# Hybrid attention/recurrence block on one core: the opening with x also laid out transposed, and four direct chunks

## The chip, the cores and the metric

The kernel runs on one core of one Trainium2 chip. A core has four engines with their own in-order instruction queues: PE (TensorE, matrix products into PSUM), DVE (VectorE, elementwise work and sums along a row), ACT (ScalarE, functions of one input with a scale and a bias per partition) and POOL (GpSimd), and SP, which only issues DMAs. The engines wait for each other through semaphores. The metric is device microseconds of one execution, the median over several runs.

## The reference

The block takes x (1024 tokens by 1024 features, fp32). In short:

```python
mod = c @ w_ada + b_ada                      # shift, scale, gate: 1024 each
h = rmsnorm(x, norm_g) * (1 + scale) + shift
proj = h @ w_in                              # 1024 x 6656
q, k, v, g_attn, xr, g_rnn, m_attn, m_rnn = split(proj)
q, k = partial_rope(q, pos), partial_rope(k, pos)
y_attn = sliding_window_attention_with_sinks(q, k, v) * silu(g_attn)
xr = causal_depthwise_conv(xr)
y_rnn = rg_lru(xr, pos) * silu(g_rnn)
merged = sigmoid(m_attn) * (y_attn @ w_ap) + sigmoid(m_rnn) * (y_rnn @ w_rp)
x = x + gate * (merged @ w_out)
return rmsnorm(x, final_g)
```

with rmsnorm(x, g) = x / sqrt(mean(x^2) + eps) * g, the mean over a token's features.

## The kernel before

Every fp32 operand of a large product is split into a high part (`h`, rounded to the format fp32r) and a low part (`l`, the rest), and the product is three: hh, hl, lh. A weight half (128 x 512) is loaded as `r`, ACT casts it to `wh` (L101, or L103 with a scale), and DVE takes the rest `wl` (L107, L109). The products need h transposed, features on the partitions, in 8 chunks of 128 features (`kc` 0 to 7), each as `hh[kc]` and `hl[kc]` over 1024 tokens in two halves.

The opening (L178 to L360) makes them. x comes in eight tiles of 128 tokens; for each, the sum of squares (four on ACT, L309, four on DVE, L311), the root (L316), the reciprocal, and the scaling of the tile (L318). PE transposes the scaled tiles (L323, 64 of them) and ACT copies them to `xT[kc]` (L325). Then for each `kc`: `modulate` (DVE, two products of a w_ss tile with the broadcast row c, each with a running sum, L220, and two small steps) gives the scale `gsc` and the shift `mods` of the 128 features; DVE applies them to `xT[kc]` (L344); ACT rounds (L347); DVE takes the rest (L349). As each chunk comes, PE adds its part of three direct output chunks (`starts`: two chunks of k and the first of q, L168), 6 matmuls of 512 columns each. In this part a scheduler sets the order of each engine's instructions, and it also pulls in matmuls of V (L1259 to L1261, 192 narrow ones in all).

From L363 on the order is that of the program text. GpSimd makes differences of the tiles `xT` (`differences`, L378), `make_operands` rounds them (L386), and then come "pairs": two output chunks by a Strassen-like scheme with 7 products of 12 matmuls (84, L505) where two direct chunks need 96. A planner with costs per step (`Load`, `background`, the slots of `at_slot`) spreads the pairs' preparation and the recurrence's steps over the pairs' products. The order of the pairs is the list `pairs`: Q[1] (query chunks), MA[0] (the first gate pair of attention), Q[2], and so on, 23 in all. Between the opening and the pairs stand the rope of k and of the first q chunk (`rope_a`, `rope_b`), V, and the second chunk of q (48 matmuls, L168).

## Time and profile before

| what | value |
|---|---|
| median of 3 runs | 944.52 us (944.16 to 946.5) |
| profiled execution | 944.47 us, span 942.5 us |
| PE busy | 908.1 us (96%) |
| DVE busy | 688.8 us (73%) |
| ACT busy | 528.8 us (56%) |
| POOL busy | 89.7 us (10%) |
| mean DMA rate | 174 GB/s |

The span is the time from the first to the last recorded instruction, and the profiled execution's own time lies 2.0 us above it. Busy shares are means over stages with different limits. In the timeline rows the columns are start, duration, engine, line, operation, output<-input, shapes and count, and in brackets the idle time of the engine just before, with what ended it. An engine's operations overlap a little at their ends, so that the distance from start to start is less than the duration shown.

### The profile page before, as it was taken

Reading aid. Unit: us, or ns where it says so; the run is one execution under the profiler, and the core shown is the slowest. Engines: PE = TensorE matmul, PEld = TensorE weight load, DVE = VectorE, ACT = ScalarE, POOL = GpSimd, SP = SyncE. Lnnn points to the kernel's source line nnn. Section 1 sums busy time; section 2 is a strip of 40 time slices with the busy share of each in tenths; the row PEclk is TensorE's granted clock in tenths of the full one; section 3 lists DMA queues with packets and bytes.
Section 4 is the critical chain, followed back from the end, with each engine's and each line's share of the span. In section 5 each row is a group of like instructions: output and inputs, shape, how many; then the busy total and the mean of one; then the engine's idle time right before and its main releaser. Section 6 shows DMA issues by size and latency. Waiting matters only on the chain.

```text
span 942.5 us, 12419 instructions
## 1 busy us (share of the span) xinstructions
PE 908.1 (96%) x4261; PEld 750.6 (80%) x4261; DVE 688.8 (73%) x1068; ACT 528.8 (56%) x1036; POOL 89.7 (10%) x129
## 2 busy tenths in 40 slices
PE   5899999999999999999999999989999999999997
PEld 3689777788888788888888778867888888887886
DVE  7977798876668955984688677888999737656522
ACT  7434654455556755866585775877888632212311
POOL 1056000000000000000000000233333300000000
PEclk9999999999999999999999999999999999999999
DMA  8923565753332433352334237897666286436321
GB/s 312 370 68 152 184 223 202 268 189 125 112 112 96 139 136 100 133 212 80 122 112 168 100 134 261 278 342 251 215 198 187 67 304 219 168 118 235 128 79 67
DMA packets 84275, 164.19 MB, mean 174 GB/s; under 512 B 12771, under 2 KB 33251, under 8 KB 84214
## 3 DMA queue, kind: packets, MB, share of 16 engines
q1 hardware_dynamic: 83350, 161.09, 49.8%
q0 software_dynamic: 720, 2.07, 0.6%
q8 instruction: 33, 0.54, 0.2%
q14 instruction: 28, 0.23, 0.1%
q10 hardware_dynamic: 144, 0.26, 0.1%
HBM read 114.00 MB, written 49.78 MB: 174 GB/s over the span
## 4 chain that ended last, share of the span: by engine, by line
PE 75%; ACT 4%; DMA 4%; DVE 4%; issue 2%; SPq 0%; POOL 0%; DVEq 0%; ACTq 0%
PE bk L505 39%; PE rp L168 12%; PE rp L1500 5%; PE pgate L778 5%; PE pmain L1500 4%; PE pmain L168 4%; PE s_ps L1016 3%; PE pv L1088 3%; PE pt L1054 1%; DMA dv<-dv_d 1%; DMA ks<-k_d 1%; DMA r<-w_rp 1%; ACT wh L101 1%; DMA r<-w_main 1%; DVE nl L390 1%
## 5 line engine op out<-in xcount | busy, mean ns | idle before, releaser
L505 PE MATMUL bk<-nh,wl 128*128 128x512 f32 x368 | 143.7, 391 | 2.0 <-DVE wl L107 1.9
L505 PE MATMUL bk<-nh,wh 128*128 128x512 f32 x368 | 143.4, 390 | 0.0
L505 PE MATMUL bk<-nl,wh 128*128 128x512 f32 x368 | 143.2, 389 | 0.0
L107 DVE TENSOR_TENSOR wl<-r,wh 128x512 fp32r<-128x512 f32 x108 | 79.1, 736 | 16.5 <-ACT wh L101 16.5
L101 ACT CAST wh<-r 128x512 fp32r<-128x512 f32 x108 | 66.5, 618 | 33.5 <-DMA r<-w_ap 11.3
L505 PEld LDWEIGHTS bk<-nh,wl 128*128 128x128 f32 x368 | 69.1, 188 | 17.7 <-DVE wl L107 3.1
L505 PEld LDWEIGHTS bk<-nh,wh 128*128 128x128 f32 x368 | 69.1, 188 | 15.2 <-ACT wh L103 0.9
L505 PEld LDWEIGHTS bk<-nl,wh 128*128 128x128 f32 x368 | 69.1, 188 | 14.3
L505 PE MATMUL bk<-hh,wl 128*128 128x512 f32 x184 | 71.7, 390 | 0.4 <-DVE wl L107 0.4
L505 PE MATMUL bk<-hl,wh 128*128 128x512 f32 x184 | 71.6, 389 | 0.0
L505 PE MATMUL bk<-hh,wh 128*128 128x512 f32 x184 | 71.6, 389 | 0.0
L107 DVE TENSOR_TENSOR wl<-ws,wh 128x512 fp32r<-128x512 f32 x80 | 54.1, 683 | 4.0 <-ACT wh L101 4.0
L101 ACT CAST wh<-ws 128x512 fp32r<-128x512 f32 x80 | 48.2, 616 | 4.8 <-DVE ws L527 3.0
L1040 ACT ACTIVATE p<-p,small 128x129 f32<-128x129 f32 x128 | 50.1, 400 | 0.0
L59 POOL DMA_DIRECT2D yh_d<-yh x1 | 0.6, 583 | 482.3 <-ACT yh L835 482.3
L505 PE MATMUL bk<-hha,wl 128*128 128x512 f32 x92 | 36.4, 395 | 5.9 <-DVE wl L107 4.4
L505 PEld LDWEIGHTS bk<-hh,wl 128*128 128x128 f32 x184 | 34.5, 188 | 7.9 <-DVE wl L107 0.8
L505 PEld LDWEIGHTS bk<-hh,wh 128*128 128x128 f32 x184 | 34.5, 188 | 7.2
L505 PEld LDWEIGHTS bk<-hl,wh 128*128 128x128 f32 x184 | 34.5, 188 | 7.1
L1016 PE MATMUL s_ps<-ks,qs 128*128 128x256 f32 (+1 forms) x256 | 37.5, 289 | 0.0
L1517 ACT ACTIVATE o<-xo 128x1024 f32<-128x1024 f32 (+2 forms) x10 | 8.9, 889 | 48.4 <-DVE xo L1516 48.4
L505 PE MATMUL bk<-hla,wh 128*128 128x512 f32 x92 | 35.9, 390 | 0.0
(338 smaller groups left out, 2231.7 us busy)
## 6 DMA issues: line engine op xcount, KB each, us to landing
r<-w_main SPq DMA_DIRECT2D x100, 256.0 KB, 4.0
wada<-w_ss SPq DMA_DIRECT2D x16, 512.0 KB, 8.6
qs<-q_d SPq DMA_DIRECT2D x16, 512.0 KB, 5.4
ks<-k_d SPq DMA_DIRECT2D x24, 192.0 KB, 4.1
xt<-x SPq DMA_DIRECT2D x8, 512.0 KB, 7.2
q_d<-rhi SPq DMA_DIRECT2D x16, 256.0 KB, 3.5
q_d<-rlo SPq DMA_DIRECT2D x16, 256.0 KB, 3.3
wg<-w_gate SPq DMA_DIRECT2D x8, 512.0 KB, 5.0
```

The source lines that it names most:

```text
L101: A.copy(dst[0][:], src)
L107: V.tensor_tensor(out=dst[1][:], in0=src, in1=f32(dst[0][:]), op=ALU.subtract)
L168: mm = T.matmul(ps[hf], ww, xx[kc][hf], start=(kc == 0 and ww is w_h and xx is xh), stop=(kc == KC - 1 and xx is xl))
L390: V.tensor_tensor(out=nl[t][:], in0=xT[t][:], in1=f32(nh[t][:]), op=ALU.subtract)
L505: W["pe"] = T.matmul(ps, ww[:, c], b[kc][xx_], start=(first and kc == 0 and i == 0), stop=(kc == 3 and i == 2), skip_group_check=not first)
L778: W["pe"] = T.matmul(ps[:, SL[hf]], ww[:, c0:c0 + P], xx_[:, SL[hf]], start=(ic == 0 and i == 0), stop=(ic == 1 and i == 2))
L1016: W["pe"] = T.matmul(o, qs[:, j, qc], ks[:, b, k0 + (0 if n else P):k0 + 256], start=(b == 0), stop=(b == 1))
L1040: A.activation(px[:, j, :], px[:, j, :], AF.Exp, bias=sm[:, 0, j:j + 1], accum_out=sm[:, 1, j:j + 1])
L1054: W["pe"] = T.transpose(pt[:, j, :], px[:, j, 0:P], ident[:])
L1088: W["pe"] = T.matmul(pv[:], b, m[:].rearrange("p j q -> p (j q)"), start=(i == 0), stop=(i == len(prods) - 1))
L1500: T.matmul(ps[:, sl], lhs[k][th][:, ts_], w[:, sl], start=(k == 0 and w is h_ and lhs is mh), stop=(k == KC - 1 and lhs is ml))
L1517: A.activation(o[:, sl], xo[:, sl], AF.Square, accum_out=fs[:, i:i + 1])
```

## The change

The input x is also handed over transposed (`x_t`), and w_ss gets a last column that holds b_ada, so that its rows have 1025 values and the sum gives the modulation with its bias. The whole opening is now in the order of the program text. The x tiles in token order serve for the sums of squares alone, all on ACT. The roots of four tiles are taken in one instruction; the reciprocals are spread over the partitions by PE (`spread`: each column of reciprocals broadcast as one operand and the identity as the other) and copied to `r_bc`. PE runs 14 and 6 dummy products (`warm`). `xT[kc]` is loaded from x_t and multiplied by `r_bc` on DVE (`norm`); ACT makes the rounded h directly from it with scale and bias (`high_h`), and then the affine tile in place (`affine`); DVE takes the rest (`low_h`). Four chunks (k twice, the two of q's first group) are multiplied as h arrives. The first gate pair MA[0] leaves the list of pairs and is multiplied directly (2 x 48 matmuls) behind V; GpSimd's differences come in another order of tiles, behind the whole opening. The third block of the recurrence (`hb` 2) loses its pauses of one slot between steps, and XR[3] is now three places behind XR[2], where MA[3] stood between.

The core of the diff:

```diff
+        load_ss(0)
+        for i in range(8):
+            load_xt(i)
+        load_t(0)
+        for i in range(3):
+            load_wh(i, 0)
+        load_ss(1)
+        load_t(1)
+        load_wh(3, 0)
+        load_t(2)
+        load_ss(2)
...
         def modulate(kc):
             for a in range(2):
-                jk = sp.tile([P, D], BF16, tag="junk2", name="jk")
+                jk = sp.tile([P, D + 1], BF16, tag="junk2", name="jk")
                 V.scalar_tensor_tensor(out=jk[:], in0=wada[kc, a][:], scalar=1.0, in1=c_bc[:],
                                        op0=ALU.mult, op1=ALU.mult,
                                        accum_out=mods[:, a * 8 + kc:a * 8 + kc + 1])
-            shf = mods[:, kc:kc + 1]
-            g1 = gsc[:, kc:kc + 1]
-            V.scalar_tensor_tensor(out=g1, in0=mods[:, 8 + kc:9 + kc],
-                                   scalar=bsc1[:, kc:kc + 1], in1=pcol(PK_NG, kc),
-                                   op0=ALU.add, op1=ALU.mult)
-            V.tensor_tensor(out=shf, in0=shf, in1=pcol(PK_BSH, kc), op=ALU.add)
-            return g1, shf
-
-        def load_start(i):
-            w = load_w(w_main[i], 0.125 if i == 2 else 1.0)
-            starts.append((w, new_ps() if i < 2 else bk[2:]))
+            V.scalar_tensor_tensor(out=gsc[:, kc:kc + 1], in0=mods[:, 8 + kc:9 + kc],
+                                   scalar=1.0, in1=pcol(PK_NG, kc), op0=ALU.add,
+                                   op1=ALU.mult)
...
+        def square(i):
+            junk = sp.tile([P, D], BF16, tag="junk", name="junk")
+            A.activation(junk[:], xt[i], AF.Square, accum_out=ss[:, i:i + 1])
+
+        def root_of(hf):
+            r1 = rr[:, hf * 4:hf * 4 + 4]
+            V.tensor_scalar(out=r1, in0=ss[:, hf * 4:hf * 4 + 4], scalar1=1.0 / D, scalar2=EPS,
+                            op0=ALU.mult, op1=ALU.add)
+            A.activation(r1, r1, AF.Sqrt)
+
+        def spread(hf):
+            r1 = rr[:, hf * 4:hf * 4 + 4]
+            V.reciprocal(r1, r1)
+            for j in range(4):
+                T.matmul(bk[2 + hf][:, j * P:(j + 1) * P],
+                         r1[:, j:j + 1].to_broadcast([P, P]), ident[:], start=True, stop=True)
+
+        def gather(hf):
+            A.copy(r_bc[:, SL[hf]], bk[2 + hf])
+
+        main = [new_ps(), new_ps()]
+
+        def warm(n):
+            for i in range(n):
+                T.matmul(main[1][0][:, :P], ident[:], ident[:], start=True, stop=True)
+
+        def norm(kc):
+            for sl in SL if kc == 0 else [slice(0, S)]:
+                V.tensor_tensor(out=xT[kc][:, sl], in0=xT[kc][:, sl], in1=r_bc[:, sl],
+                                op=ALU.mult)
+
+        def high(i, h):
+            W0[i, h] = slot()
+            cast(W0[i, h], halfw[i, h], 0.125 if i > 1 else 1.0)
+
+        def low(i, h):
+            rest(W0[i, h], halfw[i, h], 0.125 if i > 1 else 1.0)
+
+        def high_h(kc):
+            for o, i in ([(hh[kc][hf], xT[kc][:, SL[hf]]) for hf in range(2)] if kc < 4 else
+                         [(hall[kc][0], xT[kc][:])]):
+                A.activation(o, i, AF.Identity, scale=gsc[:, kc:kc + 1],
+                             bias=mods[:, kc:kc + 1])
+
+        def affine(kc):
+            A.activation(xT[kc][:], xT[kc][:], AF.Identity, scale=gsc[:, kc:kc + 1],
+                         bias=mods[:, kc:kc + 1])
+
+        def low_h(kc):
+            for o, i, h in ([(hl[kc][hf], xT[kc][:, SL[hf]], hh[kc][hf]) for hf in range(2)]
+                            if kc < 4 else [(hall[kc][1], xT[kc][:], hall[kc][0])]):
+                V.tensor_tensor(out=o, in0=i, in1=f32(h), op=ALU.subtract)
...
+        modulate(0)
+        pieces, a00 = angles()
+        for i in range(4):
+            square(i)
+        root_of(0)
+        square(4)
+        spread(0)
+        warm(14)
+        square(5)
+        gather(0)
+        turns(pieces, a00)
+        for i in range(6, 8):
+            square(i)
+        root_of(1)
+        spread(1)
+        warm(6)
+        gather(1)
+        norm(0)
+        high(0, 0)
+        high_h(0)
+        starts = [([], ps) for ps in (main[0], main[1], bk[2:], bk[:2])]
+
+        def half(i, h):
+            if (i, h) not in W0:
+                high(i, h)
+            low(i, h)
+            starts[i][0].append(W0[i, h])
+
+        half(0, 0)
+        high(1, 0)
+        high(2, 0)
+        half(1, 0)
+        half(2, 0)
+        affine(0)
+        low_h(0)
+        half(3, 0)
         for kc in range(KC):
-            if kc == 0:
-                load_start(1)
-                load_start(2)
-            else:
-                load_ss(kc)
-            with tc.issue_after(xsc.ins):
-                g1, shf = modulate(kc)
-            V.tensor_scalar(out=xT[kc][:], in0=xT[kc][:], scalar1=g1, scalar2=shf,
-                            op0=ALU.mult, op1=ALU.add)
-            for hf in range(2):
-                last = A.copy(hh[kc][hf], xT[kc][:, SL[hf]])
-            for hf in range(2):
-                V.tensor_tensor(out=hl[kc][hf], in0=xT[kc][:, SL[hf]], in1=f32(hh[kc][hf]),
-                                op=ALU.subtract)
-            if kc < 6:
+            if kc + 1 < KC:
+                modulate(kc + 1)
+                norm(kc + 1)
+                high_h(kc + 1)
+                affine(kc + 1)
+                low_h(kc + 1)
+            if kc < 4:
+                load_wh(kc, 1)
+            if kc + 3 < KC:
+                load_t(kc + 3)
+                load_ss(kc + 3)
+            if kc == 4:
+                rv = [load_half(w_v[i // 2][:, SL[i % 2]]) for i in range(4)]
+            if kc == 1:
+                table()
+            if kc == 2:
+                half(0, 1)
+            if kc == 4:
+                for i in range(1, 4):
+                    half(i, 1)
+            for terms in ("h", "l") if kc < 3 else ():
                 for w, ps in starts:
-                    mm_k(ps, w, kc, terms="h")
+                    mm_k(ps, w, kc, terms=terms)
+            if kc in (3, 4, 5):
                 for w, ps in starts:
-                    mm_k(ps, w, kc, terms="l")
-        done = None
+                    mm_k(ps, w, kc)
         for w, ps in starts:
-            with tc.issue_after(done.ins) if done else nullcontext():
-                for kc in (6, 7):
-                    done = mm_k(ps, w, kc)
-
-
-    order = ExitStack()
-    ET = mybir.EngineType
-    order.enter_context(tc.manual_schedule(engines={ET.PE, ET.Activation, ET.DVE, ET.Pool,
-                                                    ET.SP}))
+            for kc in (6, 7):
+                mm_k(ps, w, kc)
...
-                todo.extend(step + ([slots(1)] if hb < 3 else []))
+                todo.extend(step + ([slots(1)] if hb < 2 else []))
...
-    pairs = [Q[1], MA[0], Q[2], MA[1], Q[3],
-             XR[0], GR[0], GR[1], XR[1], MA[2], GR[2], MR[0], XR[2], MR[1], MR[2], MA[3],
+    pairs = [Q[1], MA[1], Q[2], MA[2], Q[3],
+             XR[0], GR[0], GR[1], XR[1], MA[3], GR[2], MR[0], XR[2], MR[1], MR[2],
...
+    for i in (3, 0, 1, 2):
...
+    kept = aside(0)
+    wv = [split(slot(), r) for r in rv]
+    ps_v = new_ps()
+    v_product(ps_v, 0)
+    rm = [load_half(w_main[C_MA + i][:, SL[j]]) for i in range(2) for j in range(2)]
     now(*part(1, rope_b, k_d))
+    now(*[rope_a(lambda hf=hf: kept[hf], hf, k_d) for hf in range(2)])
+    ps_w = new_ps()
+    v_product(ps_w, 1)
+    v_store(ps_v, 0)
     now(*part(2, rope_a, q_d[0]))
-    ps_v = new_ps()
-    v_product(ps_v, 1)
-    wq.append(split(slot(), rq[1], 0.125))
-    v_store(bk[:2], 0)
-    make_operands(0)
-    make_operands(1)
-    begin(-4, -3, -2)
-    make_operands(2)
-    v_store(ps_v, 1)
+    make_operands(3)
+    wm = [split(slot(), r) for r in rm]
+    begin(-6)
+    now(*part(3, rope_b, q_d[0]))
+    begin(-5)
+    v_store(ps_w, 1)
+    for c, ps in enumerate((bk[2:], new_ps())):
+        for kc in range(KC):
+            mm_k(ps, wm[2 * c:2 * c + 2], kc)
+        if c == 0:
+            begin(-4)
+            make_operands(0)
+            begin(-3)
+            make_operands(1)
+            begin(-2)
+            make_operands(2)
+        for hf in range(2):
+            b = blk()
+            A.activation(b, ps[hf], AF.Tanh, scale=0.5)
+            dma(sma_d[c][:, SL[hf]], b)
```

How it moves instructions, at three places. First DVE in the loop over the chunks; `hla`, `hlb` are the low halves of a chunk, `jk` the junk output of a modulation product, a higher number is a later chunk. Before, from the affine step of chunk 1 to that of chunk 2:

```order
L344 TENSOR_SCALAR xT<-xT,gsc,mods 128x1024
L220 SCALAR_TENSOR_TENSOR jk,mods<-wada,c_bc 128x1024
L228 TENSOR_TENSOR mods<-mods,pk_t 128x1
L349 TENSOR_TENSOR hla_164<-xT,hha_162 128x512
L225 SCALAR_TENSOR_TENSOR gsc<-mods,bsc_219,pk_t 128x1
L349 TENSOR_TENSOR hlb_165<-xT,hhb_163 128x512
L220 SCALAR_TENSOR_TENSOR jk,mods<-wada,c_bc 128x1024
L344 TENSOR_SCALAR xT<-xT,gsc,mods 128x1024
```

After, chunk 1 and the beginning of chunk 2 (L360 is `norm`, L383 `low_h`):

```order
L244 SCALAR_TENSOR_TENSOR jk,mods<-wada,c_bc 128x1025
L244 SCALAR_TENSOR_TENSOR jk,mods<-wada,c_bc 128x1025
L247 SCALAR_TENSOR_TENSOR gsc<-mods,pk_t 128x1
L360 TENSOR_TENSOR xT<-xT,r_bc 128x1024
L383 TENSOR_TENSOR hla_164<-xT,hha_162 128x512
L383 TENSOR_TENSOR hlb_165<-xT,hhb_163 128x512
L244 SCALAR_TENSOR_TENSOR jk,mods<-wada,c_bc 128x1025
```

Before, a modulation product of the next chunk stood between the step that ACT waits for (L344) and the one that waits for ACT (L349); now nothing stands between L360 and L383.

Second ACT in the same loop. Before, behind the transposed copies:

```order
L347 CAST hha_166<-xT 128x512
L347 CAST hhb_167<-xT 128x512
L347 CAST hha_170<-xT_191 128x512
L347 CAST hhb_171<-xT_191 128x512
L103 ACTIVATE wh<-r 128x512
L101 CAST wh<-r 128x512 x2
L347 CAST hh_174<-xT 128x512 x2
```

After, from chunk 3 to chunk 6 (L373 is `high_h`, L377 `affine`, L101 and L103 weight casts):

```order
L373 ACTIVATE hha_170<-xT,mods,gsc 128x512
L373 ACTIVATE hhb_171<-xT,mods,gsc 128x512
L377 ACTIVATE xT<-xT,mods,gsc 128x1024
L101 CAST wh<-r 128x512
L373 ACTIVATE hh_174<-xT,mods,gsc 128x1024
L377 ACTIVATE xT<-xT,mods,gsc 128x1024
L373 ACTIVATE hh_176<-xT,mods,gsc 128x1024
L377 ACTIVATE xT<-xT,mods,gsc 128x1024
L101 CAST wh<-r 128x512
L103 ACTIVATE wh<-r 128x512 x2
L373 ACTIVATE hh_178<-xT_194,mods,gsc 128x1024
```

The affine step has come over from DVE, and the second weight halves of three of the four chunks are cast behind chunk 5, ahead of chunk 6.

Third PE at the head of the program. Before, the row c is broadcast, and then come the transposes (64 in all), of which these are the first:

```order
L193 MATMUL bk_68<-c_row_t,one_row 128x512
L193 MATMUL bk_69<-c_row_t,one_row 128x512
L323 MATMUL bk_68<-ident,xt 128x128
L323 MATMUL bk_69<-ident,xt 128x128
L323 MATMUL bk_70<-ident,xt 128x128
```

After, with `spread` (L346) and `warm` (L356):

```order
L234 MATMUL bk_68<-c_row_t,one_row 128x512
L234 MATMUL bk_69<-c_row_t,one_row 128x512
L346 MATMUL bk_70<-ident,rr 128x128 x4
L356 MATMUL pmain<-ident 128x128 x14
L346 MATMUL bk_71<-ident,rr 128x128 x4
L356 MATMUL pmain<-ident 128x128 x6
L170 MATMUL pmain<-hha_158,wh 128x512
```

The 64 transposes are gone; the dummies stand ahead of the second spread in PE's queue, and the first product follows.

More of the change, by code (lines that the diff above doesn't have):

```diff
@@ L51, in tile_hybrid_block @@
 @with_exitstack
-def tile_hybrid_block(ctx, tc, x, pk, rows, posr, posi, invf, c_row, w_ss, w_gate, w_main, w_v,
+def tile_hybrid_block(ctx, tc, x, x_t, pk, rows, posr, posi, invf, c_row, w_ss, w_gate, w_main, w_v,
                       w_g, w_ap, w_rp, w_out, out):
@@ L175, in new_ps @@
         return [t[:, SL[0]], t[:, SL[1]]]
+    order = ExitStack()
+    ET = mybir.EngineType
+    order.enter_context(tc.manual_schedule(engines={ET.PE, ET.Activation, ET.DVE, ET.Pool,
+                                                    ET.SP}))
     with ExitStack() as st:
@@ L180, in tile_hybrid_block @@
         posr_t = sp.tile([P, 64], I32, name="posr_t")
-        dma(posr_t[:], posr)
         invf_t = sp.tile([P, 1], F32, name="invf_t")
-        dma(invf_t[:], invf)
-        dma(pk_t[:], pk)
-        make_identity(nc, ident)
-        c_row_t = sp.tile([1, D], F32, tag="xt", name="c_row_t", bufs=10)
-        dma(c_row_t[:], c_row)
-        one_row = sp.tile([1, P], F32, name="one_row")
-        V.memset(one_row[:], 1.0)
-        c_bc = sp.tile([P, D], F32, name="c_bc")
-        for hf in range(2):
-            T.matmul(bk[hf], one_row[:], c_row_t[:, SL[hf]], start=True, stop=True)
-            A.copy(c_bc[:, SL[hf]], bk[hf])
-        xt = []
-        starts = []
-        wada = {}
+        c_row_t = sp.tile([1, D], F32, name="c_row_t")
+        dma(c_row_t[:], c_row, A)
+        dma(posr_t[:], posr, A)
+        dma(invf_t[:], invf, A)
+        dma(pk_t[:], pk, A)
+        xt, wada, halfw, W0 = [], {}, {}, {}
         def load_ss(kc):
             for a in range(2):
-                wa_t = sp.tile([P, D], F32, tag="xt", name="wada", bufs=10)
+                wa_t = sp.tile([P, D + 1], F32, tag="xt", name="wada", bufs=9)
                 dma(wa_t[:], w_ss[a * D + kc * P:a * D + (kc + 1) * P, :])
```

204 lines of the change are left out of this document (92 added, 112 removed).

## The prediction

> **What bounds the kernel now.** I read the page first, then the busy times by stretch, then the instructions of the opening in order of time. The page:
>
> ```profile
> span 942.5 us, 12419 instructions
> PE 908.1 (96%) x4261; PEld 750.6 (80%) x4261; DVE 688.8 (73%) x1068; ACT 528.8 (56%) x1036; POOL 89.7 (10%) x129
> ```
>
> PE (TensorE) is the bound as a mean. The change lies in the first eighth of the span, so the stretches count (columns: us, then busy time and instructions of PE, PEld, DVE, ACT, POOL, granted clock, DMA share, GB/s):
>
> ```profile
> 0.00:28.20 28.20, 16.37 (x68) 11.43 (x68) 23.48 (x77) 22.00 (x44) 3.35 (x10) 1.00 0.88 326
> 28.20:61.00 32.80, 30.37 (x141) 24.21 (x139) 32.11 (x67) 10.77 (x20) 2.68 (x5) 1.00 0.61 234
> 61.00:101.00 40.00, 38.67 (x248) 34.91 (x247) 30.20 (x32) 20.83 (x33) 25.32 (x20) 1.00 0.37 132
> ...
> 480.00:645.00 165.00, 157.28 (x753) 128.74 (x751) 132.09 (x197) 116.30 (x253) 18.21 (x33) 1.00 0.64 216
> ```
>
> From 28.2 to 61 us DVE (VectorE) is busy 32.11 of 32.80 us while ACT (ScalarE) works a third of the time: in the opening it is DVE that sets the pace, and PE is fed what DVE finishes. One chunk of the old loop on DVE, from one affine step (L344) to the next:
>
> ```profile
> 32.07 0.81 DVE L344 TENSOR_SCALAR xT<-xT,gsc,mods 128x1024 f32<-128x1024 f32 x1
> 32.80 1.22 DVE L220 SCALAR_TENSOR_TENSOR jk<-wada,c_bc 128x1024 bf16<-128x1024 f32 x1
> 33.94 0.08 DVE L220 DVE_READ_ACCUMULATOR jk<-wada,c_bc 128x1 f32 x1
> 34.01 0.68 DVE L349 TENSOR_TENSOR hla<-xT,hha 128x512 fp32r<-128x512 f32 x1
> 34.61 0.21 DVE L225 SCALAR_TENSOR_TENSOR gsc<-mods,bsc,pk_t 128x1 f32<-128x1 f32 x1
> 34.74 0.68 DVE L349 TENSOR_TENSOR hlb<-xT,hhb 128x512 fp32r<-128x512 f32 x1
> 35.35 1.22 DVE L220 SCALAR_TENSOR_TENSOR jk<-wada,c_bc 128x1024 bf16<-128x1024 f32 x1
> 36.49 0.81 DVE L344 TENSOR_SCALAR xT<-xT,gsc,mods 128x1024 f32<-128x1024 f32 x1
> ...
> 60.74 1.29 DVE L349 TENSOR_TENSOR hl<-xT,hh 128x512 fp32r<-128x512 f32 x2 [0.69 <-ACT hh L347]
> ```
>
> That is 36.49 - 32.07 = 4.42 us a chunk with no gap: while ACT rounds h, DVE does a product of the next chunk's modulation (L220). The last low part of h is done at 60.74 + 1.29 = 62.0 us. PE's milestones from there (start, duration):
>
> ```profile
> 28.21 0.50 PE L168 MATMUL pmain<-hha,wh 128*128 128x512 f32 x1
> 68.03 0.28 PE L1259 MATMUL bk<-wh,hh 128*128 128x256 f32 x1
> 88.18 0.40 PE L168 MATMUL pmain<-hha,wh 128*128 128x512 f32 x1
> 99.09 0.39 PE L1306 MATMUL bk<-hha 128*128 128x512 f32 x1
> 99.32 0.39 PE L505 MATMUL bk<-hha,wh 128*128 128x512 f32 x1
> 101.19 0.50 PE L505 MATMUL bk<-hha,wl 128*128 128x512 f32 x1 [1.48 <-DVE wl L109]
> 117.85 0.39 PE L505 MATMUL bk<-hha,wh 128*128 128x512 f32 x1
> 119.82 0.50 PE L505 MATMUL bk<-hha,wl 128*128 128x512 f32 x1 [1.58 <-DVE wl L107]
> 138.81 0.39 PE L505 MATMUL bk<-hha,wh 128*128 128x512 f32 x1
> ```
>
> First product 28.21; the fourth direct chunk 88.18 to 99.09, 48 matmuls, so 0.227 us each; 168 of the 192 narrow V matmuls from 68.03 to 88.18, so 0.12 us each; the first Strassen pair starts at 99.32, the second (the gate pair that the change takes out) at 117.85, the third at 138.81. So I compare the start of "the pair after Q[1]": before, the third pair at 138.81; after, the second.
>
> **The change, part by part.**
>
> *Until the means are spread.* DMA rows, and the costs of the new steps:
>
> ```profile
> 0.81 0.39 SPq L59 DMA_DIRECT2D posr_t<-posr  x1
> 2.58 1.77 SPq L59 DMA_DIRECT2D xt<-x  x4
> 8.22 1.22 DVE L311 SCALAR_TENSOR_TENSOR junk<-xt 128x1024 bf16<-128x1024 f32 x1 [0.23 <-DMA xt<-x]
> 16.84:18.00 1.16, 1.12 (x5) 1.00 1.03 410
> 6.53 1.06 ACT L309 ACTIVATE junk<-xt 128x1024 bf16<-128x1024 f32 x1 [4.43 <-DMA xt<-x]
> 7.58 0.57 ACT L194 COPY c_bc<-bk 128x512 f32<-128x512 f32 x1
> 3.86 3.75 PE L193 MATMUL bk<-c_row_t,one_row 1*128 1x512 f32 x4 [3.86 <-DMA c_row_t<-c_row]
> 181.31 1.88 PE L877 MATMUL psg<-acc,pk_t 128*1 128x512 f32 x4
> q1 hardware_dynamic: 83350, 161.09, 49.8%
> ```
>
> The second x tile landed at 8.22 with x first issued at 2.58. The new queue starts with 512 KB tiles at about 0.81, so its second tile lands near 6.45; two w_ss tiles now stand ahead of the eight of x, so the last x tile is eight later, 0.524 MB at 410 GB/s = 1.28 us each: 16.7. Its square on ACT takes 1.05, mean, root and reciprocal about 0.6 (an estimate): 18.35. Then four fp32 matmuls of 128 columns spread the roots. Two of 512 columns took 3.75 us at the start and 1.88 late in the kernel, so one of 128 columns is 0.47 or 0.23. Ahead of them in PE's queue stand the first four and 14 dummies (from about 13 us): PE is free between 17.1 and 21.5. I take 19.2, then four at 0.3, a copy of 0.57: **G = 21.0**, the copy's end (bounds 19.9 and 24.0). w_ss rows are now 4100 bytes; whether 4 bytes travel apart no row shows. A packet means 0.498 x 942.5 x 16 / 83350 = 0.09 us, so 128 more on 16 engines cost 0 to 0.7 us a tile, 0 to 1.4 ahead of x; I take 0. The loads behind (x_t, 4.2 MB more) run at 1.57 MB, 3.8 us a chunk, faster than chunks are used.
>
> [...]
>
> *The first chunk.* Behind G, ACT has a weight cast, two rounded halves of h, two more casts and the affine step; DVE then has two low halves of h and the fourth weight's rest.
>
> ```profile
> 32.91 0.62 ACT L347 CAST hha<-xT 128x512 fp32r<-128x512 f32 x1 [3.26 <-DVE xT L344]
> 33.44 0.62 ACT L347 CAST hhb<-xT 128x512 fp32r<-128x512 f32 x1
> 91.94 3.91 ACT L389 CAST nh<-xT 128x1024 fp32r<-128x1024 f32 x4
> 93.03 4.63 DVE L390 TENSOR_TENSOR nl<-xT,nh 128x1024 fp32r<-128x1024 f32 x4 [1.15 <-ACT nh L389]
> ```
>
> A half costs ACT 0.53 (start to start), a full tile 3.91 / 4 = 0.98. So 5 x 0.53 + 0.98 = 3.6, then three DVE halves at 0.6: G + 5.5. The first product starts near G + 1.1 = 22.1, 6.1 us earlier than before.
>
> *The seven other chunks.* This is the term that decides. In the new order DVE does for each chunk: two modulation products (2 x 1.14), the small gsc step (0.13), the multiplication by the spread root (4.63 / 4 = 1.16), and then the low part of h, which can't start until ACT has made the rounded h (2 x 0.53) **and** the affine tile (0.98); nothing else of DVE stands between. So 2.41 + 1.16, a wait of 2.04 and two hand-overs (0.1 each, an estimate), and the low part, 1.2: **7.0 us a chunk** where it was 4.42. PE needs 24 x 0.227 = 5.46 for four chunks of columns, so it waits for DVE. The affine step that DVE loses (0.72) and the x scaling saved before are smaller than the new multiplication and the wait. Four rests of second weight halves add 4 x 0.6 = 2.4. The last low part of h is done at 21.0 + 5.5 + 7 x 7.0 + 2.4 = **77.9**, against 62.0. (PE also stops in chunk 4 until the second weight halves, which both engines do after chunk 5; it has 42 matmuls, 9.5 us, to catch up and over 14 us for it. That costs nothing, because chunk 7 ends later.)
>
> *To the pair after Q[1].* 38 matmuls are left at 77.9 (8.6): 86.5. V 192 x 0.12 = 23.0: 109.5. In between DVE must finish both rope parts before the weights of the direct gate pair, beside GpSimd's differences, which start behind the last chunk's step on DVE, some 16 us later than the 62 us of before:
>
> ```profile
> 72.97 1.66 POOL L384 TENSOR_TENSOR xT<-xT 128x512 f32<-128x512 f32 x1
> 73.51 1.67 DVE L431 TENSOR_TENSOR c<-c 64x512 f32<-64x512 f32 x1
> 87.85 0.68 DVE L431 TENSOR_TENSOR c<-c 64x512 f32<-64x512 f32 x1
> ```
>
> The same add took 1.67 beside GpSimd and 0.68 without. Nine or ten such operations end near the end of V; I take 1 us of PE wait (0 to 3): 110.5. The gate pair direct and the dummy at L1306 are 97 x 0.227 = 22.0: 132.5. Pair Q[1] took 117.85 - 99.32 = 18.53 with a wait of 1.48 for a weight, which now has 22 us of cover: 17.0, so 149.5; the next pair's own wait of 1.58 stays, and lay before 138.81 until now: 151.1. **12.3 us later** than 138.81. (Of it, 12 matmuls, 2.7 us, are work: 96 direct ones stand for the pair's 84.) From there the same 21 pairs and the same tail follow. The profiled execution took 944.47 us, its span and 2 around it, the median of the runs 944.52: **956.8 us**.
>
> **Rivals.**
>
> *Faster: ACT's part hides.* If DVE has work while ACT makes h, a chunk costs it 4.8 us, the last low part comes at 21.0 + 5.5 + 33.6 + 2.4 = 62.5, PE ends its four chunks at 71.1 instead of 86.5: 941.4. The point is 7.0 - 12.3 / 7 = 5.24 us a chunk. For it: the old loop was gapless, and ACT has room. Against it: the order of DVE's instructions. Chance 0.08.
>
> *The gain returns later.* From 480 to 645 us PE idles 165 - 157.3 = 7.7 us, around the last recurrence gates and the opening of attention. The recurrence now has no pauses in its third block and comes a pair earlier; if all of that idle time went, 949. For it: some of these waits are DVE's and DMA's. Against: a pair less to hide the same background work. Chance 0.12.
>
> *PE falls to the slow pace* of the first rows behind its gaps: 38 matmuls at twice 0.227, 8.6 us: 965. Against it: 119.82 came after 1.58 us of idling and its followers ran at full pace. Chance 0.07. [...]
>
> *A chunk step between 5.0 and 5.6 us,* with no difference to be told: 0.05.
>
> **How the numbers follow.** The forecast has 0.68. Its own range, from G (-1.1, +3, and 1.4 for the odd rows), hand-overs (1.4 either way), the V stretch (-1, +2) and pair waits (1.6 either way), is 952 to 962. A measurement of this kernel can tell about 0.3%, 2.8 us. Forecast, return and slow pace are all slower: 0.87, with a little of the last case 0.88; the last gives 0.04 to no change, the first rival 0.08 to faster. For 8 in 10 the range takes in the return: 947 to 962.
>
> **What would show it.** First product near 22; on DVE, in each chunk, about 2 us idle ahead of the low part of h, released by ACT's affine step; chunk steps of 7 us; V from about 86 to 110; pair Q[1] from 132. Wrong if DVE shows no such gap, or PE runs through the eight chunks without waits.

## The result, and the profile after

The changed kernel takes 977.5 us (median of 4 runs, 977.19 to 978.71), the one before 944.34 beside it (4 runs, 941.76 to 946.5): a ratio of 1.0355, 95% interval 1.0327 to 1.0382. It is slower, as forecast, but by 33 us and not by 12, and outside the range of 947 to 962. The profiled execution took 978.71 us, its span 977.0.

The page of after (span and instructions; busy time, share and count of each engine; the granted clock in 40 slices):

```profile
span 977.0 us, 12358 instructions
PE 923.0 (94%) x4265; PEld 758.9 (78%) x4265; DVE 687.4 (70%) x1021; ACT 531.9 (54%) x1021; POOL 93.0 (10%) x130
PEclk9979999999999999999999999989999999999999
```

PE is busy 15 us longer than before with four instructions more. That is a first sign that something other than work was added: in the slices with a 7 or an 8 the granted clock fell, while before's row has a 9 in all 40.

PE's milestones in after (start, duration), to be held against the six rows of before in the prediction:

```profile
22.97 0.49 PE L170 MATMUL pmain<-hha,wh 128*128 128x512 f32 x1 [0.57 <-ACT hha L373]
...
92.91 0.28 PE L1341 MATMUL pmain<-wh,hha 128*128 128x256 f32 x1
...
115.82 0.28 PE L1343 MATMUL pmain<-wh,hl 128*128 128x256 f32 x1
117.83 0.50 PE L170 MATMUL bk<-hha,wh 128*128 128x512 f32 x1 [1.73 <-ACT wh L101]
...
142.62 0.39 PE L587 MATMUL bk<-hha,wh 128*128 128x512 f32 x1
...
158.94 0.39 PE L587 MATMUL bk<-hha,wh 128*128 128x512 f32 x1
```

The first product is 5.2 us earlier than before. The four chunks end at 92.9, V at 115.9, the direct gate pair ends ahead of 142.62, and the pair after Q[1] starts at 158.94, 20.1 us later than before's 138.81. From there to the end of the span before needed 942.5 - 138.81 = 803.7 us and after needs 977.0 - 158.94 = 818.1. So the loss has **two parts: 20.1 us in the opening, and 14.4 us behind it**, where the forecast had nothing.

One chunk step on DVE in after, from one multiplication by the roots (L360) to the next, with the last low part of h at the end, and ACT's part of the same chunk:

```profile
30.26 1.22 DVE L360 TENSOR_TENSOR xT<-xT,r_bc 128x1024 f32<-128x1024 f32 x1
34.34 0.69 DVE L383 TENSOR_TENSOR hla<-xT,hha 128x512 fp32r<-128x512 f32 x1 [2.86 <-ACT xT L377]
...
38.16 1.22 DVE L360 TENSOR_TENSOR xT<-xT,r_bc 128x1024 f32<-128x1024 f32 x1
...
82.88 1.23 DVE L383 TENSOR_TENSOR hl<-xT,hh 128x1024 fp32r<-128x1024 f32 x1 [2.58 <-ACT xT L377]
```

```profile
31.52 0.81 ACT L373 ACTIVATE hha<-xT,mods,gsc 128x512 fp32r<-128x512 f32 x1 [5.19 <-DVE xT L360]
32.23 0.80 ACT L373 ACTIVATE hhb<-xT,mods,gsc 128x512 fp32r<-128x512 f32 x1
33.07 1.24 ACT L377 ACTIVATE xT<-xT,mods,gsc 128x1024 f32<-128x1024 f32 x1
```

The gap is where the forecast put it: DVE stands idle ahead of the low part, and what ends it is ACT's affine step. But it is 2.86 us long, and the step is 38.16 - 30.26 = 7.90 us, not 7.0. Both engines idle in turn here, while PE waits for both.

The late part, by busy time in stretches that begin at the same work and hold about the same number of PE's products (the first row is after, the second before; columns as in the prediction):

```profile
440.00:660.00 220.00, 203.88 (x905) 165.23 (x904) 159.28 (x217) 143.47 (x256) 12.54 (x23) 0.97 0.50 167
```

```profile
420.00:621.00 201.00, 196.54 (x902) 161.14 (x901) 150.09 (x211) 138.03 (x250) 12.60 (x23) 1.00 0.49 166
```

For about the same products, 905 and 902, after needs 220 us and before 201. PE's idle time grew from 4.5 to 16.1 us. The clock was granted at 0.97 on average for 1.00: PE was busy for 12.1 us at half of it, which is worth some 6 us more. From there on some 4 us come back: to the end of the span after needs 977.0 - 660 = 317.0 us and before 942.5 - 621 = 321.5, and that leaves the 14.4. The longest of PE's waits in after, with the pace behind the first of them:

```profile
491.33 0.50 PE L587 MATMUL bk<-nh,wl 128*128 128x512 f32 x1 [3.40 <-DVE wl L107]
491.89 0.63 PE L587 MATMUL bk<-nh,wh 128*128 128x512 f32 x1
492.32 0.63 PE L587 MATMUL bk<-nh,wl 128*128 128x512 f32 x1
...
602.25 0.50 PE L587 MATMUL bk<-hha,wl 128*128 128x512 f32 x1 [2.84 <-DVE wl L107]
609.86 1.08 PE L1098 MATMUL s_ps<-ks,qs 128*128 128x128 f32 x8 [2.10 <-DMA qs<-q_d]
...
643.60 1.22 PE L170 MATMUL rp<-hha,wh 128*128 128x512 f32 x2 [3.74 <-DVE u L658]
```

From 491.89 to 492.32 a product takes 0.43 us for 0.227. Who is late can be read only on the queues of the engines that PE waits for. ACT and DVE ahead of 491.33:

```profile
487.06 1.28 ACT L902 ACT_TABLE_LOAD   x1
488.36 1.06 ACT L902 ACTIVATE th<-th 128x1024 f32<-128x1024 f32 x1
```

```profile
489.45 1.22 DVE L905 SCALAR_TENSOR_TENSOR it<-th,it 128x1024 f32<-128x1024 f32 x1 [2.79 <-ACT th L902]
490.59 0.68 DVE L107 TENSOR_TENSOR wl<-r,wh 128x512 fp32r<-128x512 f32 x1
```

DVE had been idle for 2.79 us. The weight's rest (L107) for which PE waits stood in DVE's queue behind a step of the recurrence (L905), and that waited for ACT's root and its table load. The row of PE names L107; the cause is what stands ahead of it.

### The profile page after: what moved, and what is told of

Same layout as the page of the kernel before. It is cut to its first block, busy times and chain, and to the rows that moved or that the text cites. A ratio compares the mean times of both kernels' runs of the same rounds, so it can differ in the third digit from the quotient of the medians.

```text
span 977.0 us, 12358 instructions
## 1 busy us (share of the span) xinstructions
PE 923.0 (94%) x4265; PEld 758.9 (78%) x4265; DVE 687.4 (70%) x1021; ACT 531.9 (54%) x1021; POOL 93.0 (10%) x130
## 4 chain that ended last, share of the span: by engine, by line
PE 58%; DVE 10%; DMA 9%; ACT 8%; issue 4%; SPq 0%; POOL 0%; DVEq 0%; ACTq 0%
PE bk L587 30%; PE rp L170 9%; PE pgate L860 4%; PE rp L1595 3%; PE pmain L1595 3%; PE pv L1170 3%; PE s_ps L1098 3%; DMA wo<-w_out 3%; DMA smr<-smr_d 1%; DMA tt<-tr_d 1%; PE bk L170 1%; PE pt L1136 1%; ACT wh L101 1%; PE pmain L170 1%; DVE wl L107 1%
## 5 line engine op out<-in xcount | busy, mean ns | idle before, releaser
L587 PE MATMUL bk<-nh,wl 128*128 128x512 f32 x352 | 138.8, 394 | 4.1 <-DVE wl L107 4.1
L587 PE MATMUL bk<-nh,wh 128*128 128x512 f32 x352 | 138.6, 394 | 0.0
L587 PE MATMUL bk<-nl,wh 128*128 128x512 f32 x352 | 138.2, 393 | 0.0
L107 DVE TENSOR_TENSOR wl<-r,wh 128x512 fp32r<-128x512 f32 x109 | 83.3, 773 | 17.7 <-ACT wh L101 17.7
L101 ACT CAST wh<-r 128x512 fp32r<-128x512 f32 x109 | 66.8, 618 | 31.5 <-DMA r<-w_ap 12.2
L587 PE MATMUL bk<-hh,wl 128*128 128x512 f32 x176 | 68.9, 391 | 1.7 <-DVE wl L107 1.7
L587 PE MATMUL bk<-hh,wh 128*128 128x512 f32 x176 | 68.6, 390 | 0.4 <-ACT wh L101 0.4
L587 PE MATMUL bk<-hl,wh 128*128 128x512 f32 x176 | 68.5, 389 | 0.0
L107 DVE TENSOR_TENSOR wl<-ws,wh 128x512 fp32r<-128x512 f32 x76 | 51.7, 684 | 3.2 <-ACT wh L101 3.2
L101 ACT CAST wh<-ws 128x512 fp32r<-128x512 f32 x76 | 45.7, 615 | 4.3 <-DVE ws L609 2.6
L1098 PEld LDWEIGHTS s_ps<-ks,qs 128*128 128x128 f32 x256 | 32.4, 190 | 2.8 <-issue 2.5
```

Source lines behind the costliest of these rows:

```text
L101: A.copy(dst[0][:], src)
L107: V.tensor_tensor(out=dst[1][:], in0=src, in1=f32(dst[0][:]), op=ALU.subtract)
L587: W["pe"] = T.matmul(ps, ww[:, c], b[kc][xx_], start=(first and kc == 0 and i == 0), stop=(kc == 3 and i == 2), skip_group_check=not first)
L1098: W["pe"] = T.matmul(o, qs[:, j, qc], ks[:, b, k0 + (0 if n else P):k0 + 256], start=(b == 0), stop=(b == 1))
```

## The experiments

The theory for the opening: DVE's wait for ACT sets the chunk step, and ACT's scaled activations made it longer than forecast. The rivals: PE's slow clock, or the second weight halves. For the late part: the third block's missing pauses and the new order of the pairs crowd the recurrence's steps; the rival was that the later opening shifts everything into other phases.

### DVE's wait filled

In `ahead` the modulation runs one chunk ahead of the rest:

```diff
+        modulate(1)
         low_h(0)
...
-                modulate(kc + 1)
                 norm(kc + 1)
                 high_h(kc + 1)
                 affine(kc + 1)
+                if kc + 2 < KC:
+                    modulate(kc + 2)
                 low_h(kc + 1)
```

> The changed kernel, but the modulation of a chunk is done one chunk ahead, so that DVE has its two products to do while ACT makes the rounded h and the affine tile. If DVE's wait for ACT sets the chunk step (7.9 us in the trace of after), the step falls to the chain of one chunk, 1.16 (multiplication) + 2.86 (ACT, measured wait) + 1.2 (low part) = 5.2, or PE's 5.46: some 16 us less over seven chunks, of which the wait for the second weight halves (6.1 us in after) now shows, so 960 to 969 us. If the wait on DVE only hides behind something else (the second halves, PE's slow clock, loads), 974 to 978.

959.69 us (959.07 to 961.71), ratio to before 1.0166 (1.0147 to 1.0186): 17.8 us less than after. DVE of that run:

```profile
30.18 1.22 DVE L360 TENSOR_TENSOR xT<-xT,r_bc 128x1024 f32<-128x1024 f32 x1
...
34.27 0.69 DVE L383 TENSOR_TENSOR hla<-xT,hha 128x512 fp32r<-128x512 f32 x1 [0.26 <-ACT xT L377]
...
35.48 1.22 DVE L360 TENSOR_TENSOR xT<-xT,r_bc 128x1024 f32<-128x1024 f32 x1
```

The wait fell from 2.86 to 0.26 and the step from 7.90 to 5.30. PE's rows show what follows, and the one place where the other rival was seen:

```profile
55.96 1.22 PE L170 MATMUL pmain<-hh,wh 128*128 128x512 f32 x2 [3.46 <-ACT wh L101]
...
78.35 0.28 PE L1343 MATMUL pmain<-wh,hha 128*128 128x256 f32 x1
...
141.67 0.39 PE L589 MATMUL bk<-hha,wh 128*128 128x512 f32 x1
```

V starts 14.6 us earlier than in after and the pair after Q[1] 17.3 us earlier, within 2.9 us of before's; 12 more products on the direct gate pair are 2.7 us of these. So DVE's wait for ACT was 17.3 of the opening's 20.1 us, and the order of three lines on DVE carried it. Behind 141.67 the run needs 958.0 - 141.67 = 816.3 us, nearly as much as after: the late part isn't touched.

### ACT's price by itself

In `cast_first` ACT makes the affine tile first and rounds it by plain copies:

```diff
-                A.activation(o, i, AF.Identity, scale=gsc[:, kc:kc + 1],
-                             bias=mods[:, kc:kc + 1])
+                A.copy(o, i)
...
+        affine(0)
         high_h(0)
...
-        affine(0)
...
+                affine(kc + 1)
                 high_h(kc + 1)
-                affine(kc + 1)
```

> The changed kernel, but ACT makes the affine tile first and the rounded h from it by plain copies (0.53 us a half, 0.98 a tile) in place of a second scaled activation (0.71 a half, 1.24 a tile). If the activation with scale and bias is what made the chunk step 7.9 for the 7.0 that I forecast, DVE's wait per chunk falls from 2.86 to about 2.0 (1.24 + 0.62 + hand-over, as the second half's copy hides behind the first half's low part), the step to 7.1, and the time by 4 to 6 us: 971 to 974. If something else held the chunk back (DMA, PE's slow clock), 976 to 979.

974.81 us (972.57 to 975.83), ratio 1.0307 (1.0271 to 1.0344), 2.7 us less than after. The group that rounds the first half of a chunk, from 28 to 85 us on ACT (busy time, mean ns, then the idle time before), first of after, then of this run, and behind it this run's step on DVE:

```profile
L373 ACT ACTIVATE hha<-xT,mods,gsc 128x512 fp32r<-128x512 f32 x3 | 2.4, 813 | 13.8 <-DVE xT L360 13.8
```

```profile
L373 ACT CAST hha<-xT 128x512 fp32r<-128x512 f32 x3 | 1.9, 619 | 0.1
```

```profile
34.96 0.69 DVE L382 TENSOR_TENSOR hla<-xT,hha 128x512 fp32r<-128x512 f32 x1 [1.96 <-ACT hha L373]
...
41.97 0.69 DVE L382 TENSOR_TENSOR hla<-xT,hha 128x512 fp32r<-128x512 f32 x1 [1.96 <-ACT hha L373]
```

A pass with a scale and a bias per partition takes 0.19 us more than a plain copy of the same size, 813 for 619 ns, and on the whole chunks from 4 on 1241 for 1046. With the copies the step is 41.97 - 34.96 = 7.01 us: the mechanism held. The gain is smaller than expected, for two reasons in the trace. Chunks 4 to 7 are rounded whole, and there a DVE wait of 2.38 us stays (2.58 in after). And the first chunk's low part comes 1.5 us later (27.37 for 25.84): the affine tile now stands ahead of the first rounded half, and 0.75 us of it is that the copy of the spread roots came later in this execution (21.85 for 21.10), a step that stands ahead of the edit. Three steps by 0.9 and four by 0.2, less 1.5, are 2.0.

### The opening alone

`after_open` is after with the pair list and the pauses of before; MA[0] is a Strassen pair again.

```diff
-    pairs = [Q[1], MA[1], Q[2], MA[2], Q[3],
-             XR[0], GR[0], GR[1], XR[1], MA[3], GR[2], MR[0], XR[2], MR[1], MR[2],
+    pairs = [Q[1], MA[0], Q[2], MA[1], Q[3],
+             XR[0], GR[0], GR[1], XR[1], MA[2], GR[2], MR[0], XR[2], MR[1], MR[2], MA[3],
              XR[3], GR[3]] + GA + MR[3:]
...
-                todo.extend(step + ([slots(1)] if hb < 2 else []))
+                todo.extend(step + ([slots(1)] if hb < 3 else []))
...
-    for c, ps in enumerate((bk[2:], new_ps())):
-        ... (the direct pair; the operands stay)
```

> The changed opening alone: after with the pair list and the pauses of before (MA[0] is a Strassen pair again, not multiplied directly). The direct pair's 97 products no longer cover the making of the operands (8 casts and 8 rests, some 8 to 10 us), and a pair of 84 stands for 96. If the loss behind the opening belongs to pauses and order, it goes: 977.5 - 14.4 - 2.7 + 8 = 968 (964 to 972), with PE's idle time from the last gates to the end like that of before (some 8 us). If it belongs to the opening's lateness, it stays: 980 to 985.

975.36 us (972.93 to 977.11), ratio 1.0327 (1.0303 to 1.0351). Slower than expected, but its two halves come apart cleanly. PE's rows at Q[1]'s start, and in the late part:

```profile
125.28 0.79 PE L587 MATMUL bk<-hha,wh 128*128 128x512 f32 x1 [4.09 <-ACT wh L103]
130.15 0.80 PE L587 MATMUL bk<-hha,wl 128*128 128x512 f32 x1 [4.08 <-DVE wl L109]
...
560.53 0.50 PE L587 MATMUL bk<-nh,wl 128*128 128x512 f32 x1 [0.63 <-DVE wl L107]
...
590.87 0.50 PE L587 MATMUL bk<-nh,wl 128*128 128x512 f32 x1 [1.25 <-DVE wl L107]
```

The late waits are before's, 0.63 and 1.25 in place of 3.40 and 2.84: behind the opening this run loses 0.5 us against before (972.8 - 189.39 = 783.4, from a wait that both have at the start of the fourth pair, against 942.5 - 159.55 = 782.95). The whole loss of 30 us lies ahead of it. At that wait it stands 189.39 - 159.55 = 29.8 us behind before, where after, with the direct pair, was 20.1 behind at the start of the pair before it. Without the direct pair nothing covers the making of the operands, and PE stops twice for 4 us, with a slower pace behind each stop (0.79 and 0.80 us for the first products, where those behind the two late waits took 0.50). So the direct pair saves the new opening about 10 us, and what it costs comes in the late part, with the pauses and the order that were changed along with it.

### The late part on the old opening

Three runs take parts of the late change to the kernel before: `before_nopause` the pauses of the third block, `before_nopause_b1` those of the second instead, `before_late` the third block's pauses and the shorter way from XR[2] to XR[3].

```diff
-                todo.extend(step + ([slots(1)] if hb < 3 else []))
+                todo.extend(step + ([slots(1)] if hb < 2 else []))          # before_nopause, before_late
+                todo.extend(step + ([slots(1)] if hb in (0, 2) else []))    # before_nopause_b1
...
-    pairs = [Q[1], MA[0], Q[2], MA[1], Q[3],
+    pairs = [Q[1], MA[0], Q[2], MA[1], MA[3], Q[3],                         # before_late
-             XR[0], GR[0], GR[1], XR[1], MA[2], GR[2], MR[0], XR[2], MR[1], MR[2], MA[3],
+             XR[0], GR[0], GR[1], XR[1], MA[2], GR[2], MR[0], XR[2], MR[1], MR[2],
```

> The kernel before, with only the pauses of the third recurrence block taken out (hb < 2 for hb < 3). If the missing pauses cause the loss behind the opening (14.4 us between the pair after Q[1] and the end in after), this loses 5 to 14 us: 950 to 958, with a PE stall on a weight's low part of 3 us or more near the third block's steps and a slow clock behind it. If the order of the pairs or the lateness of the opening is the cause, 943 to 946.

> The kernel before with the pauses taken out of the second recurrence block (hb 1) in place of the third. If missing pauses cost by themselves, because a block's steps then queue ahead of weight casts and rests on ACT and DVE, this block costs what the third one did (948.9 - 944.4 = 4.5 us): 947 to 950, with a PE stall of about 3 us on a weight's rest in that block's stretch. If the third block's loss came from its neighbourhood (the fourth block right behind, which has no pauses either), 944 to 945.

> The kernel before, with the pauses out and XR[3] three places behind XR[2] (MA[3] moved ahead of Q[3]); 23 pairs and the opening of before. If pauses and order together cause the late loss, 954 to 962; if the order matters and the pauses do not, the same while the run with the pauses alone stays at 944; if it is the changed opening that moves the late part into other phases, 943 to 946 in both.

| run | median us | ratio to before (95%) |
|---|---|---|
| before_nopause | 948.9 | 1.005 (1.0033 to 1.0068) |
| before_nopause_b1 | 948.18 | 1.0042 (1.0025 to 1.0059) |
| before_late | 957.86 | 1.0148 (1.0126 to 1.017) |

`before_late` loses 13.5 us with the opening untouched, against the 14.4 of after. Its waits are after's, in the same places and of nearly the same length; the one of 3.74 us is missing:

```profile
471.17 0.50 PE L505 MATMUL bk<-nh,wl 128*128 128x512 f32 x1 [3.37 <-DVE wl L107]
...
582.87 0.50 PE L505 MATMUL bk<-hha,wl 128*128 128x512 f32 x1 [2.84 <-DVE wl L107]
...
590.15 1.08 PE L1016 MATMUL s_ps<-ks,qs 128*128 128x128 f32 x8 [1.77 <-DMA qs<-q_d]
```

So pauses and order carry the late loss, and the later opening does not: that rival has fallen. Of the 13.5 us, 4.5 come with the pauses alone, the other 9 with the new order on top of them. That order puts XR[0] to XR[2] a place later as well as XR[3] nearer to XR[2]; neither was run alone, so which of the two matters is not shown.

The two runs with pauses taken from one block were also to show *where* a missing pause costs, and there the expectation failed. The new stall of `before_nopause` stands at 540.00 us, when PE has done the fourth block's last gates (from 522.70 to 528), and that of `before_nopause_b1` at 527.66, in the fourth block as well, not in the second. Ahead of each row of PE is shown the step of the fourth block that stood ahead of the awaited rest on DVE:

```profile
538.06 1.28 DVE L799 SCALAR_TENSOR_TENSOR rz<-rz,pk_t,rbig 128x1024 f32<-128x1024 f32 x1 [3.13 <-ACT rz L793]
...
540.00 0.72 PE L505 MATMUL bk<-nh,wl 128*128 128x512 f32 x1 [3.31 <-DVE wl L107]
```

```profile
524.58 1.23 DVE L816 SCALAR_TENSOR_TENSOR th<-rz,th 128x1024 f32<-128x1024 f32 x1 [5.52 <-ACT rz L813]
...
527.66 0.50 PE L505 MATMUL bk<-hha,wl 128*128 128x512 f32 x1 [2.63 <-DVE wl L107]
```

The block that lost its pauses runs without a longer stall in these two runs; it ends sooner, and the fourth block, which never had pauses, starts some 5 to 7 us earlier than before (its gates at 509 and 511 us for 516). In both stalls one of the fourth block's steps, waiting for ACT, kept DVE from the awaited rest. That its new place among the casts and rests brought this about is the likely reason, but it is not shown. Which rule of the planner brings a given step ahead of a given rest stays open.

### Some pauses back

No run has all the pauses with 22 pairs; that they don't fit is a reckoning, not shown. `some_pauses` puts one behind every third step of the third block:

```diff
-                todo.extend(step + ([slots(1)] if hb < 2 else []))
+                todo.extend(step + ([slots(1)] if hb < 2 or (hb == 2 and i % 3 == 2) else []))
```

> The changed kernel with a pause behind every third step of the third recurrence block (all of them don't fit into 22 pairs). If it is the missing pauses that make the stalls from 480 to 605 us (3.40, 0.85, 0.83, 0.72 and 2.84 us on a weight's rest, and the half pace behind them), some go: 1 to 5 us less, 972 to 976. If only the place of XR[3] matters, 977 to 978; if the later end of the block hits the opening of attention, 979 to 983.

975.85 us (974.31 to 977.24), ratio 1.033 (1.0311 to 1.0349), 1.65 us less than after's median, with the ranges meeting. The first stall fell from 3.40 to 1.56 us; the 2.84 of the fourth block stayed as it was. So pauses do act on their own block's stall here, but this is a small part of the 14.4 us.

### The bank of the last product

The wait of 3.74 us at 643.60 is in none of the runs with 23 pairs. Pairs take their PSUM banks by the parity of their place. With 22 pairs the last product lies in the bank that the next stage's first accumulator takes over. `parity` swaps the banks:

```diff
-            p.place(7 * i, i % 2, i == len(pairs) - 1)
+            p.place(7 * i, (i + 1) % 2, i == len(pairs) - 1)
```

> The changed kernel with the two alternating PSUM banks of the pairs swapped (the parity of a pair's place plus one). With 22 pairs for 23 the last pair's last product lies in bk[1], which the next stage's first accumulator (rp) takes over, and PE waits 3.74 us there for DVE's add (L658) and runs at half pace behind it (12 products or so at 0.43 for 0.23 us, 2.3 us). If the parity is the cause, both go: 6 us less, 970 to 973. If DVE is only crowded there, 976 to 978.

976.27 us (975.3 to 979.46), ratio 1.0337 (1.0291 to 1.0383): no difference from after that can be told. The wait is gone, so its cause is shown. But PE now waits later, as before did, with 1.39 and 1.14 us in the rows below:

```profile
658.86 0.47 PE L1170 MATMUL pv<-phc,vs 128*128 128x512 f32 x1 [1.39 <-DVE small L1117]
...
670.32 0.47 PE L1170 MATMUL pv<-phc,dv 128*128 128x512 f32 x1 [1.14 <-DVE small L1128]
```

In this stretch PE waits for attention's own steps on DVE; the 3.74 us had largely stood in the place of these waits. The expectation of 6 us counted one wait and its slow pace, and not what was late next.

### The gains together

`ahead_parity` joins the two edits, `ahead_parity_halves` also prepares the second weight halves of chunks 1 to 3 ahead of chunk 5's step, and `ahead_parity_pauses` is `ahead_parity` with the pauses of `some_pauses`.

```diff
-            if kc == 4:
-                for i in range(1, 4):
-                    half(i, 1)
...
+            if kc == 4:                     # now ahead of norm(kc + 1)
+                for i in range(1, 4):
+                    half(i, 1)
```

> The modulation one chunk ahead (959.7 us) and the banks swapped. The two waits lie in different stages, so the gains should add: 959.7 - 6 = 953.5 (952 to 956). If the parity does nothing, 959 to 961.

> As the run before, with the second weight halves of chunks 1 to 3 prepared ahead of chunk 5's step for behind it. In the run with the modulation ahead PE idled 3.46 us for them at 56 us and ran some 3 us at half pace. If PE sets the end of the four chunks there, 4 to 5 us less than the run before; if DVE's last low part (68.4 us, and 38 products behind it) sets it, nothing to 1 us less, because PE only waits later.

> Modulation one chunk ahead, banks swapped, and a pause behind every third step of the third block: the gains as far as found, to see whether they add. 959.1 less what the run with some pauses gains on after (1 to 5): 954 to 958; if the pauses only move the stalls, 959 to 961.

959.11 us (1.0141; 1.0107 to 1.0176), 961.02 (1.0165; 1.013 to 1.02) and 956.27 (1.0118; 1.0097 to 1.0139). The parity gives nothing here either. The earlier halves remove PE's wait of 3.46 us, and PE waits in other places, for h and then for the weights of the direct gate pair:

```profile
59.10 0.72 PE L170 MATMUL pmain<-hl,wh 128*128 128x512 f32 x2 [1.03 <-DVE hl L383]
...
69.00 0.73 PE L170 MATMUL pmain<-hl,wh 128*128 128x512 f32 x2 [1.32 <-DVE hl L383]
...
102.66 0.50 PE L170 MATMUL bk<-hha,wh 128*128 128x512 f32 x1 [1.73 <-ACT wh L101]
```

With them DVE's last low part sets the end of the chunks, and V starts at 77.74 us for 79.39 in `ahead_parity`: with the modulation ahead the second halves did cost 1.7 us at that place. But the time doesn't reach the end. PE then waits 1.73 us for the gate weights, and the pair after Q[1] starts at 143.79 for 141.57. The run is 1.9 us slower than `ahead_parity`, with ranges that don't meet, which neither case of the expectation allowed for. `ahead_parity_pauses` is the fastest kernel with the new opening, as expected, and still 1.2% slower than before; none beats it. What is left is mostly the late part.

## Why the prediction was wrong

**What held.** The sign, and the mechanism that was to decide: DVE idle in each chunk ahead of the low part, released by ACT's affine step. G came at 21.7 (21.0 forecast), the first product at 22.97 (22.1). That G is so near is in part luck: the forecast let the last x tile set it, but from the third square on ACT waited for no tile, and its squares, some 1.2 us each, ended at 19.2, so that the reciprocals came at 19.86 and not at 18.35. The last 38 products took 92.9 - 84.1 = 8.8 us (8.6), V 23.0 (23.0). The second weight halves cost nothing at the end: PE's last wait in the chunks, 1.34 us at 84.16, is for the low part of h.

**The chunk step was mis-sized: 7.9 us for 7.0.** The step that failed is "(2 x 0.53) and the affine tile (0.98)". Those were rows of plain casts of before (L347, L389), and the new instructions have a scale and a bias per partition. Measured: 0.71 and 0.84 from start to start for the halves and 1.24 for the tile, and DVE's multiplication and modulation came out 0.3 us longer together. From chunk 4 on, with whole tiles, the step was some 7.6. The seven steps with their rests took 84.1 - 27.65 = 56.5 us for 51.4, and the first chunk was done 1.2 us late, so that the last low part of h came at 82.88 + 1.23 = 84.1 and not at 77.9. V ended 6.4 us late for that reason. The run with plain copies shows the step at 7.01. Two small terms were the author's estimates, with no row behind them: the hand-overs, taken at 0.1 us each, were 0.04 to ACT (31.48 to 31.52) and 0.03 back to DVE (34.31 to 34.34) in after, and mean to reciprocal, taken at 0.6, took 0.65 (19.21 to 19.86).

**From V to the pair after Q[1]: 43.0 us for 41.6.** The wait for the gate weights was 1.73 and 0.80 for the 1 us taken, and the products behind it ran in part at half pace: the granted clock was 0.92 from 120 to 140 us, 1.6 us. Pair Q[1] gave 2.3 us back (16.3 for 18.6). Together with the chunks these make 7.2 of the 7.8 us by which 158.94 missed 151.1.

**"From there the same 21 pairs and the same tail follow" is the step that failed worst: 14.4 us.** The missing pauses and the new place of XR[3] were named in the change and priced at nothing. They appear only in the rival "The gain returns later", as a way to lose idle time, with "a pair less to hide the same background work" as an argument against it, and never as a new loss. That rival also says that the recurrence "comes a pair earlier". Counted from the pair after Q[1], XR[3] keeps its place and XR[0] to XR[2] come a pair later: the first block's gates start at 290.8 us for 251.3, 39.5 later, of which 20.1 are the opening. The trace of before held the warning: of the 7.7 us of PE idle time from 480 to 645 us, 3.3 lay around the fourth block, the one block without pauses, released by weight rests; the other 4.4 lay in the opening of attention, for DMA and DVE. A second block without pauses and a shorter way between the two should have been priced from there, and upward. `before_late` shows 13.5 us of it on the old opening.

**The range.** It had no term for this, and none for the chunk step beyond its hand-overs. Its upper end isn't the sum of its terms either: 3 + 1.4 + 1.4 + 2 + 1.6 us above 956.8 are 966, not 962, while the lower end is such a sum. The measured 977.5 lies outside both.

**The rivals.** "ACT's part hides" did not happen, but `ahead` made it happen: 959.7 against the 941.4 written there. Of the difference 12.6 us lie behind the pair after Q[1] (816.3 us for before's 803.7) and 6.0 ahead of it (141.67, where the rival's numbers give 151.1 - 15.4 = 135.7). "PE falls to the slow pace" had a chance of 0.07 and was placed ahead of the last 38 products. There the pace stayed full, with a granted clock of 1.00 from 84.16 to 92.9 us. It came in the waits ahead of them, where DVE was late anyhow, and in the late part, where it cost some 6 us.

## What to carry to other kernels

Price a moved operation by the form it will have: on ACT the same tile cost 0.81 us with a scale and a bias per partition and 0.62 as a copy, and a chain that a second engine waits for multiplied that by the chunks. When one engine waits for another in a loop, put the next round's independent work between them first: three lines in another order were worth 17.8 us here. And where a change removes pauses, or moves a stage closer to the next, look at what stands ahead of the weights in the in-order queues, and not only at whether the work is the same.

## What the runs showed of the hardware

PE's clock fell after gaps as short as 1.04 us, and not after each longer one. PE's rows in after, from the chunks of the opening: a gap that no slower pace followed, then twice a gap and a product some 1.5 us behind it, and last the granted clock (PEclk, third number from the end) of the 3.4 us behind the second gap:

```profile
32.38 0.50 PE L170 MATMUL pmain<-hha,wh 128*128 128x512 f32 x1 [1.99 <-ACT hha L373]
...
40.28 0.50 PE L170 MATMUL pmain<-hha,wh 128*128 128x512 f32 x1 [1.68 <-ACT hha L373]
41.75 0.63 PE L170 MATMUL pmain<-hhb,wl 128*128 128x512 f32 x1
...
50.90 0.50 PE L170 MATMUL pmain<-hla,wh 128*128 128x512 f32 x1 [1.04 <-DVE hla L383]
52.50 0.63 PE L170 MATMUL pmain<-hhb,wh 128*128 128x512 f32 x1
```

```profile
41.32:44.73 3.41, 3.41 (x9) 2.63 (x8) 2.45 (x5) 2.49 (x3) 0.80 (x1) 0.50 1.03 416
```

Gaps of 1.68 and 1.04 us, in a stretch in which PE worked 5.5 us of every 7.9, were followed by 3.4 us at half pace (0.63 long, for 0.39), while the 1.99 us ahead of them and the 2.84 us at 602.25 were not followed by any at once. The 3.40 and 3.74 us of the late part were, and so were the 2.10 us at 609.86.

So the length of a gap alone doesn't tell what follows. By the granted clock of this trace the stretches at half pace, up to PE's last product, begin at 41.32, 51.56, 61.80, 119.83, 491.88, 611.35 and 642.07 us, which are whole multiples of 3.413 us apart (10.24 is three of them), and last 3.41, 6.83 or 10.24 us. Why they begin there is not shown.
